# Small products of both heads claim their PSUM banks together, with new bank pools and a port rule in the planner

## Chip, cores and metric

One core of a Trainium2 chip runs the whole program. The metric is the device time of one execution in microseconds (us). The engines are TensorE (PE, its weight loads PEld), VectorE (DVE), ScalarE (ACT), GpSimd (POOL) and the DMA queue of SyncE (SP).

## What is computed

One mixer layer over 1024 tokens of width 1024, batch 1, all in fp32. An RMS norm and one wide projection feed two branches, a chunked gMLP and an RWKV-7 recurrence of 16 heads of 64; both are gated, merged and projected out.

```python
p = rms_norm(x, norm_pre_g) @ w_in
pa, pb, pg = p[..., :3072], p[..., 3072:7296], p[..., 7296:]
ya = gmlp_branch(pa, ...)      # u * (W_s LN(v) + b) * silu(z), blocks of 128 tokens
yb = rwkv7_branch(pb, ...)     # S_t = S_{t-1} diag(w_t) + (S_{t-1} (-kk_t)) (kk_t a_t)^T + v_t k_t^T ; o_t = S_t r_t
merged = sigmoid(pg[..., :1024]) * (ya @ w_branch_a) + sigmoid(pg[..., 1024:]) * (yb @ w_branch_b)
x = x + rms_norm(merged @ w_out, norm_post_g)
```

## The kernel before

**Dense products.** Large products are 128 x 128 weights against 512 columns. Each fp32 operand is split into a high and a low part (`whi`, `wlo`; `hm` for the activations), and three passes hi*hi, hi*lo, lo*hi are added in a `ps` bank. They run at the lowest priority, `DENSE`, in any gap of TensorE.

**Half-units.** `half_unit` handles the recurrence for one pair of heads and one half of the tokens: 8 pairs times 2 halves, 16 half-units, each with 8 chunks of 64 tokens. Head E lies in partitions 0 to 63, head O in 64 to 127. The small products of a half-unit stay in plain fp32, where one product is two records of TensorE in the trace (a transpose is one):

- `pg<-W,BK`: per chunk and head a 64-row product, each head into a bank of its own, four chunks to a bank; so two pairs of banks per half-unit, two times eight products. VectorE masks the banks into `Pm`, `BA` and `W`.
- An inversion of triangular blocks: `Pm` goes through DRAM into `B`, GpSimd runs a loop of 62 instructions (`qt<-B,Q` and `Q<-Q,qt`), the result comes back through DRAM as `N`, VectorE transposes it into `Pm` in four pieces, and 16 `N,Pm` and 16 `Pm,N` products finish it. Each of these two sets fills one `pm` bank.
- `pg<-con,v`, `pg<-con,BK`, `pg<-con,W`: centring and transposes over 128 rows.
- `X,Pm`: two times eight products; both heads write the same bank, at their own partitions.
- `BA,X`: like `W,BK`, two pairs of banks.
- `pc<-Z,W`: a chain of eight steps over the chunks, each carried on by ScalarE and VectorE; then `po<-W,Z`, 16 products into one `po` bank, which ends the half-unit on TensorE.
- Sums over heads (`head_sum`): ScalarE makes `sh`, GpSimd makes `sl` from it, TensorE multiplies both with `bdr`.

Buffers decide how far half-units overlap: `W` has 5 (two per half-unit, written at its beginning and read until its `po`), `Pm` and `BA` 2, `BK`, `B`, `Q`, `N` and `X` 1. Of the eight PSUM banks `ps` has 3, `pg` 2, `pm`, `po` and `pc` 1 each.

**Order.** `Sched` records all operations, then `flush` lists them per engine: it repeats choosing the ready operation that can start earliest, by costs from `cost`, and of equals the one with the smaller priority (`CHAIN` 0, `INV` 1, `PREP` 2.5, `LATE` 4, `DENSE` 9). `when` gives the time from which an operation's buffers are free. The engines then run their lists in that order, and wait on semaphores. Products of a `group_of` become ready together; `claim` names tiles that an operation must have before it starts.

**Stages.** Projections with `gp` tiles; the recurrent stage, in which the column tiles of the projections for the next heads and some of the `w_a` products are the dense work; the rest of `w_a`; and the last products (`product`, seven block products twice), for which VectorE and GpSimd split operands.

Of the kernel before, what the change touches and what calls it, by code (L numbers as in the profile page):

```python
# [11 lines left out]
F32 = mybir.dt.float32  # L12
F32R = mybir.dt.float32r
AF = mybir.ActivationFunctionType
# [4 lines left out]
P = 128  # L19
# [42 lines left out]
class Sched:  # L62
# [17 lines left out]
    def __init__(self, nc, tc=None, plan=None):  # L80
        self.nc, self.tc, self.plan = nc, tc, plan
        self.calls, self.cls, self.prio = [], [], 0
        self.ntile = self.nflush = 0
        self.PE, self.DVE, self.ACT, self.POOL, self.SP = (Queue(self, e) for e in self.ENGINES)
        self.names = {}
        self.group, self.bufs, self.slot = [], {}, []
        self.shape, self.dtype, self.used = [], [], []
        self.ops, self.orders, self.done = [], [], 0
        self.heirs, self.places = {}, {}
        self.hist, self.ends = {}, []  # L90
        self.free = dict.fromkeys(self.ENGINES, 0.0)
        self.hw = self.dq = 0.0
        self.table, self.array = None, (P, P)
        self.start, self.made = [], {}
# [27 lines left out]
    def call(self, eng, op, a, k):  # L122
# [8 lines left out]
        i = len(self.ops)  # L131
# [14 lines left out]
        if eng == "PE":  # L146
            size = (P, P) if op == "transpose" else (a[1].shape[0], a[1].shape[-1])
        self.ops.append((eng, deps, tiles, dur, (self.prio, i), table, size, op))

    cache = {}  # L150

    def region(self, ap, shape):

        sig = (tuple(shape), ap.offset, tuple(map(tuple, ap.ap)))
        if sig not in self.cache:
# [10 lines left out]
            self.cache[sig] = tuple(masks)  # L166
        return self.cache[sig]

    def cost(self, eng, op, a, k, outs, ins):
# [23 lines left out]
        if eng == "DVE":  # L193
            if op == "transpose":
                return 335, None, 0
            if op == "reciprocal":
                return 6.3 * n + 62, None, 0
            if op in ("bn_stats", "bn_aggr"):
                return (62 + ins[0].free_size()) / .96, None, 0
            if op in ("tensor_scalar", "tensor_copy") and not psum:  # L200
                n /= 2
            return (62 + n) / .96 + 63 * ptr, None, 0
# [9 lines left out]
    def flush(self):  # L212
# [38 lines left out]

        def when(t, i):
            for v in ops[i][2]:
                if v in where:
# [4 lines left out]
                    continue  # L259
                g = self.group[v]  # L260
                if self.bufs[g][1] and nxt[g][-1] != v:
                    return None
                s = state.setdefault(g, [])
                for h in [h for h in self.heirs.get(g, ()) if not nxt.get(h)]:
                    self.heirs[g].remove(h)
                    self.places[g] += [(h, k) for k in range(len(state[h]))]
                    s += state[h]
                if len(s) < self.bufs[g][0]:
                    continue
                f = [lastend[u] for u in s if not users.get(u)]  # L270
                if not f:
                    return None
                t = max(t, min(f))
            return t
# [5 lines left out]
        while len(order) < n - b0:  # L280
# [18 lines left out]
            ready[e] = [x for x in ready[e] if x[1] != i]  # L299
            eng, deps, tiles, dur, prio, table, size = ops[i][:7]  # L300
            for v in tiles:
# [18 lines left out]
            else:  # L320
# [6 lines left out]
                self.start[i] = s  # L327
                self.free[e] = ends[i] = s + dur
            order.append(i)
            for v in tiles:  # L330
# [53 lines left out]
def half_unit(S, I, rw, dram, bank, p, h, r, k0, v, zz, uh, ul, bdr, xw, xa, Z, KI, vec, con, hv, eps, yb):  # L384
# [76 lines left out]
    for c4 in range(2):  # L461
        cc = slice(4 * c4, 4 * c4 + 4)
        ps2 = [bank([P, 4, P], "pg") for _ in range(2)]
        with S.group_of():
            for j in range(4):
                for ps, e, hp in zip(ps2, (0, 1), (E, O)):
                    mm(ps[:, j, :], BK[hp, 4 * c4 + j, :], W2[c4][hp, j, :, e, :], start=True, stop=True,
                       claim=[Pm, BA])
        for ps, e, hp, other in zip(ps2, (0, 1), (E, O), (O, E)):
# [30 lines left out]
    py = bank([P, 8, 32], "pm")  # L500
    for c in range(8):
        for a in (0, 64):
            mm(py[a:a + 64, c, :], Pm[a:a + 32, c, :], N[a:a + 32, c, :], start=True, stop=True)
    Y = N
    V.tensor_scalar(Y, py, con[:, C_LOW:C_LOW + 1], None, op0=ALU.mult)
    p2 = bank([P, 8, 32], "pm")
    for c in range(8):
        for a in (0, 64):
            mm(p2[a:a + 32, c, :], Y[a:a + 64, c, :], Pm[a:a + 64, c, 32:64], start=True, stop=True)
    for a in (0, 64):  # L510
# [28 lines left out]
    for c4 in range(2):  # L539
# [5 lines left out]
        act(X[:, cc, :], px, AF.Copy)  # L545
    for c4 in range(2):
        cc = slice(4 * c4, 4 * c4 + 4)
        px = bank([P, 4, P], "pg")
        with S.group_of():
            for j in range(4):  # L550
                for hp in (E, O):
                    mm(px[hp, j, :], Pm[hp, 4 * c4 + j, :], X[hp, 4 * c4 + j, :], start=True, stop=True)
        act(X[:, cc, :], px, AF.Copy)

    for c4 in range(2):
        cc = slice(4 * c4, 4 * c4 + 4)
        ps2 = [bank([P, 4, P], "pg") for _ in range(2)]
        with S.group_of():
            for j in range(4):
                for ps, hp in zip(ps2, (E, O)):  # L560
                    mm(ps[:, j, :], X[hp, 4 * c4 + j, :], BA[hp, 4 * c4 + j, :], start=True, stop=True)
        for ps, e in zip(ps2, (0, 1)):
# [56 lines left out]
def trunk(S, enter, I, out):  # L619
# [31 lines left out]
    def bank(shape, name):  # L651
        bufs = {"ps": 3, "pg": 2, "pm": 1, "po": 1, "pc": 1}[name]
        return psum.tile(shape, F32, name=name, bufs=bufs, fifo=name in ("pc", "po", "pm"))

# [658 lines left out]
```

## Time and profile before

| | us |
|---|---|
| three runs, median (lowest to highest) | 1537.02 (1535.17 to 1548.76) |
| the profiled execution, time | 1538.7 |
| its span, first to last instruction | 1536.6 |
| TensorE busy in the span | 1433.5 (93%) |
| VectorE busy | 1058.2 (69%) |
| GpSimd busy | 905.6 (59%) |
| ScalarE busy | 732.6 (48%) |

Busy time of TensorE runs from a product's start to its modelled end, and products overlap, so the start-to-start distance in a timeline is what a product costs. A group of rows by line (`L127` is the recording helper, so nearly all operations carry it) is told apart by its tiles, `out<-in`. A wait is named after the operation that came last.

### The profile page before, as it was taken

How to read it: one execution, taken by the hardware profiler on the slowest of the kernel's cores; microseconds unless marked ns; L12 is line 12 of the kernel's file. 1: busy time of each engine (PE TensorE's matmuls, PEld its weight loads, DVE VectorE, ACT ScalarE, POOL GpSimd, SP SyncE). 2: the span in 40 equal slices, each digit the busy share in tenths (PEclk: the TensorE clock that was granted, in tenths of full speed). 3: DMA queues.
4: the chain of work that ended last, by engine and by line, in shares of the span. 5: the costliest groups of instructions: out<-in, count | busy, mean ns of one | idle time of the engine just before them, and what ended most of it. 6: DMA issues, size and time to landing. Idle time of an engine off the chain costs nothing. (4 is left out here: it accounts for less than half of the span.)

```text
span 1536.6 us, 23389 instructions
## 1 busy us (share of the span) xinstructions
PE 1433.5 (93%) x8390; PEld 1141.3 (74%) x8390; DVE 1058.2 (69%) x1764; ACT 732.6 (48%) x1334; POOL 905.6 (59%) x1405
## 2 busy tenths in 40 slices
PE   5999999999999999999999999989999999888796
PEld 3788788888887777777777777767777777666585
DVE  7868677753328576876867768658586745398977
ACT  5625443433336455655655555446555543043343
POOL 5554677764432665664664655647646562199686
PEclk9999999999999999999997999979999999999898
DMA  6104234433322111211122111111215744644032
GB/s 221 53 1 181 84 138 140 141 126 110 110 103 67 48 40 49 63 53 46 39 59 63 52 39 52 53 42 45 62 53 181 249 153 153 217 132 135 22 110 110
DMA packets 99155, 145.76 MB, mean 95 GB/s; under 512 B 42336, under 2 KB 52704, under 8 KB 99040
## 3 DMA queue, kind: packets, MB, share of 16 engines
q1 hardware_dynamic: 99040, 144.28, 28.7%
q8 instruction: 66, 1.08, 0.3%
q14 instruction: 49, 0.40, 0.1%
HBM read 106.49 MB, written 37.75 MB: 94 GB/s over the span
## 5 line engine op out<-in xcount | busy, mean ns | idle before, releaser
L127 PE MATMUL ps<-hm,whi 128*128 128x512 f32 x1616 | 549.0, 410 | 6.6 <-ACT whi L127 6.6
L127 PEld LDWEIGHTS ps<-hm,whi 128*128 128x128 f32 x1616 | 306.0, 193 | 71.1 <-ACT whi L127 7.0
L127 PE MATMUL ps<-hm,wlo 128*128 128x512 f32 x808 | 330.9, 410 | 0.0
L127 POOL TENSOR_TENSOR qt<-B,Q 128x60 f32<-128x60 f32 (+24 forms) x496 | 197.1, 397 | 83.0 <-DMA Q<-in_q_dram 34.7
L127 POOL TENSOR_TENSOR Q<-Q,qt 128x60 f32<-128x60 f32 (+24 forms) x496 | 183.3, 370 | 37.2
L127 PEld LDWEIGHTS ps<-hm,wlo 128*128 128x128 f32 x808 | 155.3, 192 | 33.2 <-issue 2.3
L127 ACT ACTIVATE whi<-raw 128x1024 fp32r<-128x1024 f32 x64 | 67.6, 1057 | 122.0 <-PE ps L127 69.5
L127 ACT ACT_TABLE_LOAD x69 | 88.5, 1283 | 1.9 <-PEq L1296 0.7
L127 PE MATMUL pg<-pg,ring 128*128 128x512 f32 x360 | 86.5, 389 | 0.0
L127 PE MATMUL pg<-W,BK 64*128 64x128 f32 (+1 forms) x521 | 76.5, 305 | 10.2 <-DVE W L127 4.6
L127 PEld LDWEIGHTS pg<-W,BK 64*128 64x128 f32 (+1 forms) x521 | 63.5, 203 | 29.5 <-issue 15.6
L127 POOL TENSOR_TENSOR wlo<-raw,whi 128x1024 fp32r<-128x1024 f32 x18 | 43.4, 2411 | 61.9 <-ACT whi L127 61.9
L127 PEld LDWEIGHTS pg<-pg,ring 128*128 128x128 f32 x360 | 67.6, 188 | 14.0
L127 ACT ACTIVATE Z<-pc,gc 64x64 f32<-64x64 f32 x120 | 36.7, 306 | 78.6 <-PE pc L127 71.8
L127 DVE TENSOR_TENSOR wlo<-raw,whi 128x1024 fp32r<-128x1024 f32 x46 | 58.2, 1265 | 20.3 <-ACT whi L127 19.6
L127 POOL TENSOR_TENSOR sl<-k,sh 128x512 fp32r<-128x512 f32 x16 | 23.9, 1496 | 74.7 <-ACT sh L127 74.7
L127 DVE TENSOR_SCALAR Z<-pc,gc 64x64 f32<-64x64 f32 x120 | 34.9, 291 | 43.5 <-ACT Z L127 28.6
L127 PE MATMUL pg<-BA,X 64*128 64x128 f32 x512 | 57.8, 289 | 0.3
L127 PEld LDWEIGHTS pg<-BA,X 64*128 64x128 f32 x512 | 46.9, 187 | 14.7 <-issue 7.9
L127 PE MATMUL ps<-pg,hm 128*128 128x512 f32 x192 | 53.1, 433 | 4.7 <-ACT hm L127 4.0
L127 ACT ACTIVATE X<-pg 128x512 f32<-128x512 f32 x64 | 37.4, 591 | 39.7 <-PE pg L127 39.3
L127 DVE TENSOR_TENSOR W<-pg,KI 128x256 f32<-128x256 f32 x64 | 26.9, 420 | 38.6 <-PE pg L127 38.4
(860 smaller groups left out, 3262.6 us busy)
## 6 DMA issues: line engine op xcount, KB each, us to landing
raw<-in_w_in_dram SPq DMA_DIRECT2D x65, 512.0 KB, 3.3
B<-bs_d SPq DMA_DIRECT2D x64, 128.0 KB, 2.6
hm<-ya_d SPq DMA_DIRECT2D x32, 256.0 KB, 5.4
raw<-in_w_a_dram SPq DMA_DIRECT2D x12, 512.0 KB, 3.9
sv<-sv_d SPq DMA_DIRECT2D x8, 512.0 KB, 3.3
ya_d<-th SPq DMA_DIRECT2D x8, 512.0 KB, 2.6
ya_d<-sv SPq DMA_DIRECT2D x8, 512.0 KB, 2.6
yb_d<-oc SPq DMA_DIRECT2D x16, 256.0 KB, 2.2
```

Of the source, the lines that this page charges most:

```text
L127: self.calls.append(lambda: getattr(e, op)(*a, **k))
```

## The change

1. `W,BK` and `BA,X` products claim both banks of their pair; a product cannot start until both are free, so that the list can take the heads in turn. `when` now asks for as many free buffers as an operation needs of a pool.
2. Both sets of `N,Pm` and `Pm,N` products become groups. `X,Pm` claims both of its banks and runs as one group.
3. The pools `pm` and `po` are dropped, `pg` has 4 banks and serves all three.
4. The planner knows the SBUF port that VectorE and GpSimd share: `shares` tells which operations use it (every GpSimd operation but a memset; on VectorE two SBUF inputs, or a copy or scalar operation within SBUF), and in the plan such an operation waits for the other engine's last one. No instruction comes of it. `tensor_tensor_scan` gets a cost of its own.

```diff
+        self.port = {"DVE": 0.0, "POOL": 0.0}
...
+    def shares(self, eng, op, outs, ins):
+
+        if eng == "POOL":
+            return op != "memset"
+        if eng != "DVE":
+            return False
+        sb = [x for x in ins if x.free_size() > 1 and self.group[self.names[x.tensor.name]][0] != "psum"]
+        if op in ("tensor_scalar", "tensor_copy"):
+            return len(sb) == 1 and self.group[self.names[outs[0].tensor.name]][0] != "psum"
+        return len(sb) > 1
...
+            if op == "tensor_tensor_scan":
+                return 2.23 * n, None, 0
...
         def when(t, i):
+            want = {}
...
+                want[g] = want.get(g, 0) + 1
                 if self.bufs[g][1] and nxt[g][-1] != v:
                     return None
+            for g, m in want.items():
...
-                if len(s) < self.bufs[g][0]:
+                m -= max(0, self.bufs[g][0] - len(s))
+                if m <= 0:
                     continue
-                f = [lastend[u] for u in s if not users.get(u)]
-                if not f:
+                f = sorted(lastend[u] for u in s if not users.get(u))
+                if len(f) < m:
                     return None
-                t = max(t, min(f))
+                t = max(t, f[m - 1])
+            if ops[i][8]:
+                t = max(t, self.port["POOL" if ops[i][0] == "DVE" else "DVE"])
             return t
...
+                if port:
+                    self.port[e] = s + dur
...
                     mm(ps[:, j, :], BK[hp, 4 * c4 + j, :], W2[c4][hp, j, :, e, :], start=True, stop=True,
-                       claim=[Pm, BA])
+                       claim=[Pm, BA, *ps2])
...
-    for c in range(8):
-        for a in (0, 64):
-            mm(py[a:a + 64, c, :], Pm[a:a + 32, c, :], N[a:a + 32, c, :], start=True, stop=True)
+    with S.group_of():
+        for c in range(8):
+            for a in (0, 64):
+                mm(py[a:a + 64, c, :], Pm[a:a + 32, c, :], N[a:a + 32, c, :], start=True, stop=True)
...
-    for c4 in range(2):
-        cc = slice(4 * c4, 4 * c4 + 4)
-        px = bank([P, 4, P], "pg")
-        with S.group_of():
-            for j in range(4):
-                for hp in (E, O):
-                    mm(px[hp, j, :], Pm[hp, 4 * c4 + j, :], X[hp, 4 * c4 + j, :], start=True, stop=True)
-        act(X[:, cc, :], px, AF.Copy)
+    px2 = [bank([P, 4, P], "pg") for _ in range(2)]
+    with S.group_of():
+        for c in range(8):
+            for hp in (E, O):
+                mm(px2[c // 4][hp, c % 4, :], Pm[hp, c, :], X[hp, c, :], start=True, stop=True, claim=px2)
+    for c4, px in enumerate(px2):
+        act(X[:, 4 * c4:4 * c4 + 4, :], px, AF.Copy)
...
-                    mm(ps[:, j, :], X[hp, 4 * c4 + j, :], BA[hp, 4 * c4 + j, :], start=True, stop=True)
+                    mm(ps[:, j, :], X[hp, 4 * c4 + j, :], BA[hp, 4 * c4 + j, :], start=True, stop=True, claim=ps2)
...
-        bufs = {"ps": 3, "pg": 2, "pm": 1, "po": 1, "pc": 1}[name]
-        return psum.tile(shape, F32, name=name, bufs=bufs, fifo=name in ("pc", "po", "pm"))
+        name = {"pm": "pg", "po": "pg"}.get(name, name)
+        bufs = {"ps": 3, "pg": 4, "pc": 1}[name]
+        return psum.tile(shape, F32, name=name, bufs=bufs, fifo=name == "pc")
```

The lists of TensorE show what comes of it. The first place is the `W,BK` products of the eighth half-unit, before; `pg_540` and `pg_541` are the banks of head E and head O for the first four chunks, `pg_542` the bank of head E for the last four.

```order
L127 MATMUL pg_540<-W_4870,BK_4880 128x128 x4
L127 MATMUL ps_539<-hm_1206,wlo_1077 128x512
L127 MATMUL ps_539<-hm_1208,whi_1076 128x512
L127 MATMUL ps_539<-hm_1212,whi_1076 128x512
L127 MATMUL pg_541<-W_4870,BK_4880 128x128 x4
L127 MATMUL ps_539<-hm_1208,wlo_1077 128x512
L127 MATMUL ps_539<-hm_1209,whi_1076 128x512
L127 MATMUL ps_539<-hm_1214,whi_1076 128x512
L127 MATMUL pg_542<-W_4891,BK_4880 128x128 x4
```

The same place of the change, the last four chunks (`pg_547` head E, `pg_548` head O):

```order
L128 MATMUL pg_547<-W_4902,BK_4890 128x128
L128 MATMUL pg_548<-W_4902,BK_4890 128x128
L128 MATMUL pg_547<-W_4902,BK_4890 128x128
L128 MATMUL pg_548<-W_4902,BK_4890 128x128
L128 MATMUL pg_547<-W_4902,BK_4890 128x128
L128 MATMUL pg_548<-W_4902,BK_4890 128x128
```

Before, four products of one head stand in a row, with dense products between the heads; now the heads take turns. The first four chunks (`pg_536`, `pg_537`) stand about 50 rows earlier in the list, in the same alternation but for one product that comes some rows later.

The second place is `BA,X` of the eleventh half-unit, before; `pg_689` is head E's bank, `pg_691` head O's.

```order
L127 MATMUL pg_688<-X_5028,Pm_5004 64x128 x8
L127 MATMUL pg_689<-BA_5005,X_5028 128x128 x4
L127 MATMUL ps_677<-hm_1217,whi_1100 128x512
L127 MATMUL ps_677<-hm_1220,whi_1100 128x512
L127 MATMUL ps_677<-hm_1217,wlo_1101 128x512
L127 MATMUL ps_690<-hm_1189,whi_1103 128x512
L127 MATMUL ps_690<-hm_1190,whi_1103 128x512
L127 MATMUL pg_691<-BA_5005,X_5028 128x128 x4
```

And of the change, where `pg_699` and `pg_701` are banks of head E, `pg_700` and `pg_702` of head O:

```order
L128 MATMUL pg_697<-X_5033,Pm_5004 64x128 x8
L128 MATMUL ps_693<-hm_1207,whi_1106 128x512
L128 MATMUL ps_693<-hm_1209,whi_1106 128x512
L128 MATMUL ps_693<-hm_1207,wlo_1107 128x512
L128 MATMUL ps_693<-hm_1210,whi_1106 128x512
L128 MATMUL pg_699<-BA_5003,X_5033 128x128
L128 MATMUL pg_700<-BA_5003,X_5033 128x128
L128 MATMUL pg_699<-BA_5003,X_5033 128x128
```

All sixteen `BA,X` products of the half-unit now follow each other in turn, where before they were four runs of four.

## Rows read from the trace of the kernel before

**Rows 1.** Windows: length, then busy (instructions) by engine, PEclk, DMA, GB/s.

```profile
0.00:482.00 482.00, 460.18 (x2035) 377.27 (x2035) 305.07 (x465) 209.55 (x389) 266.42 (x195) 0.99 0.33 115
482.00:1290.00 808.00, 769.32 (x5507) 601.21 (x5507) 559.26 (x1089) 436.76 (x784) 472.57 (x1104) 0.96 0.24 73
1290.00:1339.00 49.00, 40.47 (x175) 31.85 (x172) 18.79 (x22) 11.57 (x14) 4.75 (x3) 0.93 0.68 234
1339.00:1537.00 198.00, 163.49 (x685) 130.97 (x683) 175.08 (x189) 74.74 (x149) 161.85 (x103) 0.92 0.30 100
```

**Rows 2.** Groups of PE by shape: records | busy us, mean ns | idle before.

```profile
L127 PE MATMUL pg<-W,BK 64*128 64x128 f32 x512 | 73.9, 304 | 10.2 <-DVE W L127 4.6 <-ACT KI L127 2.1 <-DVE BK L127 1.8
L127 PE MATMUL pg<-BA,X 64*128 64x128 f32 x512 | 57.8, 289 | 0.3
L127 PE MATMUL pg<-X,Pm 64*64 64x128 f32 x512 | 33.6, 277 | 1.1 <-ACT KI L127 0.5 <-DVE bon L127 0.3 <-DVE sq L127 0.2
L127 PE MATMUL pm<-N,Pm 32*64 32x32 f32 x512 | 30.7, 236 | 9.5 <-DVE Pm L127 9.3
L127 PE MATMUL pm<-Pm,N 64*32 64x32 f32 x512 | 13.4, 211 | 0.0
```

**Rows 3.** Timeline of PE in the eleventh half-unit: start us, us, operation, records.

```profile
1037.35 1.09 PE L127 MATMUL pg<-X,Pm 64*64 64x128 f32 x16 [0.24 <-DVE sq L127]
1038.37 1.16 PE L127 MATMUL pg<-BA,X 64*128 64x128 f32 x8
1039.46 0.73 PE L127 MATMUL ps<-hm,whi 128*128 128x512 f32 x2
1040.03 0.39 PE L127 MATMUL ps<-hm,wlo 128*128 128x512 f32 x1
1040.26 0.63 PE L127 MATMUL ps<-hm,whi 128*128 128x512 f32 x2
1040.82 1.16 PE L127 MATMUL pg<-BA,X 64*128 64x128 f32 x8
```

**Rows 4.** Timeline of PE, a run of `W,BK` in the sixteenth half-unit.

```profile
1204.92 1.24 PE L127 MATMUL pg<-W,BK 64*128 64x128 f32 x16
1206.09 1.15 PE L127 MATMUL po<-W,Z 128*64 128x64 f32 x32
```

**Rows 5.** Timeline of PE, a run of `N,Pm` in the third half-unit.

```profile
632.35 2.00 PE L127 MATMUL pm<-N,Pm 32*64 32x32 f32 x32
634.28 0.50 PE L127 MATMUL pg<-sh,bdr 128*128 128x512 f32 x1
```

**Rows 6.** Longest waits of PE, 482 to 1290: us in total, times, longest.

```profile
PE pg L127 <- POOL sl L127: 10.1, 8, 3.5
PE pm L127 <- DVE Pm L127: 9.3, 14, 2.2
```

**Rows 7.** Timeline of POOL (two rows) and of DVE at one time.

```profile
695.18 0.35 POOL L127 TENSOR_TENSOR qt<-B,Q 128x68 f32<-128x68 f32 x1
...
696.02 1.22 POOL L127 TENSOR_TENSOR qt<-B,Q 128x64 f32<-128x64 f32 x1
...
695.81 1.23 DVE L127 TENSOR_TENSOR wlo<-raw,whi 128x1024 fp32r<-128x1024 f32 x1 [0.44 <-ACT whi L127]
```

**Rows 8.** Timeline of PE: the loop from the eighth to the tenth half-unit.

```profile
904.08 1.15 PE L127 MATMUL po<-W,Z 128*64 128x64 f32 x30
...
922.34 1.91 PE L127 MATMUL pg<-W,BK 64*128 64x128 f32 x16
...
981.79 1.61 PE L127 MATMUL pm<-N,Pm 32*64 32x32 f32 x32
...
1004.62 1.15 PE L127 MATMUL po<-W,Z 128*64 128x64 f32 x32
```

**Rows 9.** Timeline of PE between the last half-unit and the last products.

```profile
1325.49 1.22 PE L127 MATMUL ps<-hm,whi 128*128 128x512 f32 x2 [6.57 <-ACT whi L127]
...
1338.87 0.85 PE L127 MATMUL ps<-BA,xa 128*128 128x512 f32 x3
```

More of the change, by code (lines that the diff above doesn't have):

```diff
@@ L147, in call @@
             size = (P, P) if op == "transpose" else (a[1].shape[0], a[1].shape[-1])
-        self.ops.append((eng, deps, tiles, dur, (self.prio, i), table, size, op))
+        self.ops.append((eng, deps, tiles, dur, (self.prio, i), table, size, op, self.shares(eng, op, outs, ins)))
     cache = {}
@@ L299, in flush @@
             ready[e] = [x for x in ready[e] if x[1] != i]
-            eng, deps, tiles, dur, prio, table, size = ops[i][:7]
+            eng, deps, tiles, dur, prio, table, size, _, port = ops[i]
             for v in tiles:
@@ L506, in half_unit @@
     p2 = bank([P, 8, 32], "pm")
-    for c in range(8):
-        for a in (0, 64):
-            mm(p2[a:a + 32, c, :], Y[a:a + 64, c, :], Pm[a:a + 64, c, 32:64], start=True, stop=True)
+    with S.group_of():
+        for c in range(8):
+            for a in (0, 64):
+                mm(p2[a:a + 32, c, :], Y[a:a + 64, c, :], Pm[a:a + 64, c, 32:64], start=True, stop=True)
     for a in (0, 64):
@@ L545, in half_unit @@
         act(X[:, cc, :], px, AF.Copy)
-    for c4 in range(2):
-        cc = slice(4 * c4, 4 * c4 + 4)
-        px = bank([P, 4, P], "pg")
-        with S.group_of():
-            for j in range(4):
-                for hp in (E, O):
-                    mm(px[hp, j, :], Pm[hp, 4 * c4 + j, :], X[hp, 4 * c4 + j, :], start=True, stop=True)
-        act(X[:, cc, :], px, AF.Copy)
+    px2 = [bank([P, 4, P], "pg") for _ in range(2)]
+    with S.group_of():
+        for c in range(8):
+            for hp in (E, O):
+                mm(px2[c // 4][hp, c % 4, :], Pm[hp, c, :], X[hp, c, :], start=True, stop=True, claim=px2)
+    for c4, px in enumerate(px2):
+        act(X[:, 4 * c4:4 * c4 + 4, :], px, AF.Copy)
     for c4 in range(2):
```

## Prediction

> **What bounds the kernel now.** First the busy time by stage [rows 1]. The program has four stretches: projections that need no small products (0 to 482 us), the recurrent stage with the small products of 16 half-units (482 to 1290), what is left of the dense products of `w_a` (1290 to 1339), and the last products (1339 to the end). In the recurrent stage TensorE is busy 769 of 808 us, VectorE 559, ScalarE 437, GpSimd 473. So TensorE carries the stage: it is idle 38.7 us, and its granted clock of 0.96 there means that about 8% of the stage ran at the lower of the two levels, which lost about 32 us. Dense products have the lowest priority in the planner and fill every gap, so TensorE's work, not one dependency, is the first thing to count.
>
> Next the groups of TensorE by shape [rows 2]. Each of the kinds listed there has 512 records, two for a product, so 256 products in 16 half-units. `pg<-W,BK` costs 73.9 us, `pg<-BA,X` 57.8, but `pg<-X,Pm`, which also streams 128 columns through 64 rows, only 33.6. The timeline shows why [rows 3, 4]. In `X,Pm` the heads alternate, since both write one bank: eight products start at 1037.35 and the next kind starts at 1038.37, 1.02 us. `BA,X` writes a bank for each head, and here the program has four products of one head alone: 1038.37 to 1039.46, 1.09 us for four; the other head's four start at 1040.82. Where the banks happened to be free together the heads alternate there too: eight `W,BK` products take 1204.92 to 1206.09, 1.17 us [rows 4].
>
> **The change part by part.** *Banks claimed at once.* The order of the built programs gives the counts. Products that follow one of the same head inside a run: `W,BK` 146 before and 0 after, `BA,X` 72 and 0. A broken bank pair has six such steps, so these are 24 + 12 = 36 broken pairs of 64. A broken pair costs two runs of 1.09 us, each with a lead-in: the two dense products that start at 1040.26, at the 0.23 us from 1040.03 to 1040.26, would let the next start at 1040.72, and it starts at 1040.82, so 0.10 us [rows 3]. That is 2 x 1.19 = 2.38. An alternating run costs 1.17 + 0.10 = 1.27. Each pair saves 1.11 us, 36 pairs 40 us.
>
> *Fewer runs.* Entries into one of the six small kinds from another array shape fall from 189 to 134. Of these 55, 36 are counted above. For the other 19 no row shows a run's fixed cost alone; it lies between the 0.10 us lead-in and the 0.5 us by which a run of four (1.09) exceeds half an alternating run of eight (0.58). I take 0.3, so 6 us (2 to 10).
>
> *`N,Pm` as a group.* The order has 98 same-head steps in it before and none after. It costs 30.7 us, `Pm,N`, alternating already, 13.4 [rows 2]; one half-unit's run lasts from 632.35 to 634.28, 1.93 us [rows 5]. Of the 17.3 us difference 9.3 are waits for VectorE's four transposes [rows 6], which a group only gathers into one wait ahead of it. The gain is between 0 and 8 us; I take 5, nearer the upper end because runs without a wait are slow as well.
>
> That `N,Pm` gains at all although both heads write one bank is read from `X,Pm`: one bank, eight products, 1.02 us [rows 3]. The Trainium skill, TensorEngine Tiling (Array Packing), section Restrictions and Gotchas, says that different row tiles cannot access the same PSUM bank at the same time. By that rule this gain would be nothing and the sum 46 in place of 51. The trace disagrees with it here, since alternating in one bank costs no more than alternating over two.
>
> *`X,Pm` over two banks in one run, `pm` and `po` out of the `pg` pool.* The bank count stays at eight. `X,Pm` is entered 23 times for 20, under 1 us. The dense and last stages keep their products. Cost nothing, hidden by TensorE's own stream; if a bank were missing, the price would show as a wait of TensorE for an evacuation, and its two longest waits are of another kind [rows 6].
>
> *The shared port in the planner.* It adds no instruction, but reorders VectorE and GpSimd everywhere. That the two do block each other is seen at 695.81: VectorE's `wlo` runs 1.23 us, and GpSimd's `qt` that starts at 696.02 takes 1.22 in place of 0.35 [rows 7]. The old plan did not know this, so TensorE's order expects GpSimd early and waits 10.1 us for `sl` and 9.3 for the transposes behind GpSimd's loop [rows 6]. A truer plan can give back up to these 19 us; a worse order can cost as much. Outside the recurrent stage it could add or remove one wait of the last stage, where TensorE idles 34.5 us [rows 1]; I take both as 0, with about 10 us either way.
>
> *Sum.* 40 + 6 + 5 = 51 us of TensorE's work. As an upper bound, `W,BK` and `BA,X` at the price of `X,Pm` give 40.3 + 24.2, with 8 for `N,Pm` 72; the lower bound is the first term alone, 40. TensorE is busy 95% of the stage, so I let it all reach the end, with idle time and clock loss as they are. The profiled execution took 1538.7 us, 1.7 over the median of 1537.0: 1487.7 by its own time, **1486** against the median.
>
> **The rivals.**
>
> *The chain of half-units sets the pace.* A half-unit needs the `W` buffers of the one two before it. Their loop reads: last product of one, `po`, at 904.08; `W,BK` of the second next at 922.34; `N,Pm` at 981.79 behind GpSimd's triangular inversion; `po` at 1004.62 [rows 8]. That is 100.5 us for two half-units, the same as the stage's 808 / 8 = 101, so the loop is as tight as TensorE's work is. If it holds its length, freed TensorE time is filled with dense products only. The order shows what then happens: 739 dense products stand behind the last `po`, 846 before, so 107 x 0.23 = 24.6 us leave the tail; the `w_a` remainder there shrinks from 160 products to 53. The recurrent stage stays at 808: 1514 against the profiled run, **1512** against the median. For it: the loop's length. Against it: small products are on the loop as well, 51 / 16 = 3.2 us a half-unit. The Trainium skill, the same page, section Performance Considerations, warns that evacuation of PSUM becomes the bottleneck once tiling has made TensorE faster, which would end here too. The trace bears that out little: VectorE is busy 69% of the stage [rows 1].
>
> *The waits go as well.* If the truer plan removes the waits of [rows 6], 51 + 19 = 70 us: **1467**.
>
> *The new order stretches the loop: slower.* Between the first and the last `W,BK` product of a half-unit stand 10 dense products before and 30 after (means of the order): +20 x 0.23 = 4.6 us. Between the last and `N,Pm` 131 and 165: +7.8. From there to `po` 6 fewer: -1.4. With 3.2 us off for the small products, a loop grows by 7.8 us if the order sets its length; eight loops +62, less 24.6 of the tail, +37: **1574**. It is slower than before by over 1% once loops grow by 5 us (8 x 5 = 40 = 24.6 + 15.4). Against it: `W,BK` to `N,Pm` took 59 us from first to first [rows 8], far more than the dense products in it, so the inversion sets it and the added ones fill time in which TensorE had slower small products and waits.
>
> **How the numbers follow.** Forecast (1470 to 1505) 60%; waits go too (1455 to 1470) 12%; the loop sets the pace (1505 to 1521) 16%; gains and losses of the order cancel (1521 to 1552) 7%; slower rival 5%. The range 1458 to 1518 takes in the 72 us bound and most of the loop's case, and leaves out about 2 in 10. One per cent, 15 us, is about what a measurement of this kernel can tell from no change: faster 0.87, same 0.08, slower 0.05.
>
> **What would show it.** In the profile after: `pg<-W,BK` and `pg<-BA,X` near 36 to 45 us each, in runs of 16 records of about 1.2 us; `N,Pm` near 25; TensorE's busy time in the recurrent stage lower by about 51 less the 24 us of dense products moved in; from the last `po` to the first of the last products about 25 us in place of 49 [rows 9], with the 6.57 us wait for a `w_a` load perhaps still in it. The waits for `sl` show whether the port rule matters. If the small products shrink as said but TensorE's idle time grows by 25 us or more, the loop was the bound. If `W,BK` stays above 60 us, alternation was not what made it dear and the sum is wrong.

## The result: 1487.46 us, and the profile after

The changed kernel takes 1487.46 us (median of four runs, 1484.92 to 1489.99). The kernel before, timed again beside it, takes 1541.04; the ratio is 0.9649, 95% interval 0.9596 to 0.9703. The forecast was 1486. One execution of the kernel before and one of e12 below, which took more than twice as long as the others (3413 and 3147 us), are left out of every figure here.

The profile after by stage, in the four stretches of [rows 1] and with the same columns; the borders are the first `W,BK`, the last `po` (now `pg<-W,Z`) and the first of the last products:

```profile
0.00:494.30 494.30, 462.16 (x2037) 375.69 (x2037) 297.32 (x466) 215.11 (x392) 270.84 (x195) 0.99 0.32 112
494.30:1256.60 762.30, 718.06 (x5613) 567.20 (x5614) 565.91 (x1102) 438.41 (x786) 458.25 (x1104) 0.96 0.28 85
1256.60:1269.40 12.80, 12.80 (x65) 10.55 (x61) 5.99 (x7) 7.98 (x11) 4.21 (x3) 1.00 0.18 68
1269.40:1487.30 217.90, 164.68 (x685) 131.69 (x683) 164.67 (x190) 75.45 (x149) 154.10 (x103) 0.88 0.34 112
```

The recurrent stage is 45.7 us shorter and the remainder of `w_a` 36.2, but the projections are 12.3 us and the last products 19.9 us longer: -49.7 in all between the two profiled executions (the medians differ by 53.6). The total that was forecast is thus made of gains larger than forecast and of losses that were not forecast.

TensorE's groups by shape, which answer to [rows 2]:

```profile
L128 PE MATMUL pg<-W,BK 64*128 64x128 f32 x512 | 41.7, 287 | 0.0
L128 PE MATMUL pg<-BA,X 64*128 64x128 f32 x512 | 35.1, 280 | 0.0
L128 PE MATMUL pg<-X,Pm 64*64 64x128 f32 x512 | 34.3, 275 | 0.0
L128 PE MATMUL pg<-N,Pm 32*64 32x32 f32 x512 | 22.9, 233 | 7.9 <-DVE Pm L128 7.7
```

`W,BK` gave 32.2 us, `BA,X` 22.7, `N,Pm` 7.8: 62.7. `X,Pm`, now one run over two banks, costs what it did (33.6). The timeline of the eleventh half-unit shows the new form, to be held against [rows 3]:

```profile
1016.23 1.74 PE L128 MATMUL pg<-X,Pm 64*64 64x128 f32 x26
1017.89 0.73 PE L128 MATMUL ps<-hm,whi 128*128 128x512 f32 x2
1018.46 0.39 PE L128 MATMUL ps<-hm,wlo 128*128 128x512 f32 x1
...
1019.02 2.06 PE L128 MATMUL pg<-BA,X 64*128 64x128 f32 x32
1021.00 0.51 PE L128 MATMUL ps<-hm,whi 128*128 128x512 f32 x1
```

All sixteen `BA,X` products of the half-unit start at 1019.02 and the next dense product at 1021.00: 1.98 us, 2.08 with the lead-in of 0.10 that the run has here as well. Before they were four runs of 1.09 with a lead-in of 0.10 each, 4.76 us.

TensorE's waits in the recurrent stage, answering to [rows 6] (us in total, times, longest):

```profile
PE pg L128 <- ACT sh L128: 26.8, 7, 8.4
PE pg L128 <- DVE Pm L128: 7.7, 6, 4.6
...
PE pg L128 <- POOL sl L128: 1.7, 2, 1.1
```

The waits for `sl` (10.1 before) are nearly gone, and waits for ScalarE's `sh` have come. The longest of them on TensorE:

```profile
858.02 1.16 PE L128 MATMUL pg<-W,BK 64*128 64x128 f32 x16
859.12 0.50 PE L128 MATMUL ps<-hm,wlo 128*128 128x512 f32 x1
859.45 0.39 PE L128 MATMUL pg<-sl,bdr 128*128 128x512 f32 x1
868.20 0.79 PE L128 MATMUL pg<-sh,bdr 128*128 128x512 f32 x1 [8.36 <-ACT sh L128]
```

Behind `W,BK` stand one dense product and one of `sl`, and then TensorE's list has nothing before the product of `sh`: it has no dense product at this place, though it has more of them later (the next starts at 873.84).

In the last stage TensorE's waits are 40.3 us in five, where they were 21.0 in three; the two longest after, and the longest before:

```profile
PE ps L128 <- POOL wlo L128: 21.0, 1, 21.0
PE ps L128 <- DVE raw L128: 11.2, 1, 11.2
```

```profile
PE ps L127 <- DVE wlo L127: 9.8, 1, 9.8
```

And GpSimd, which makes the `wlo` of the longest, stands still for 11.57 us ahead of it: the next operation in its list waits for VectorE's `Pm`.

```profile
1372.39 2.86 POOL L128 TENSOR_TENSOR hm<-hm,hm 128x512 f32<-128x512 f32 x2 [11.57 <-DVE Pm L128]
...
1383.26 1.71 POOL L128 TENSOR_TENSOR wlo<-hm,wlo 128x512 fp32r<-128x512 f32 x1
```

### The profile page after: what moved, and what is told of

Same layout as the page of the kernel before. It is cut to its first block, busy times and chain, and to the rows that moved or that the text cites. A ratio compares the mean times of both kernels' runs of the same rounds, so it can differ in the third digit from the quotient of the medians.

```text
span 1487.3 us, 23327 instructions
## 1 busy us (share of the span) xinstructions
PE 1357.7 (91%) x8390; PEld 1085.1 (73%) x8390; DVE 1033.9 (70%) x1764; ACT 737.0 (50%) x1336; POOL 887.4 (60%) x1405
## 5 line engine op out<-in xcount | busy, mean ns | idle before, releaser
L128 PE MATMUL ps<-hm,whi 128*128 128x512 f32 x1616 | 538.5, 405 | 2.2 <-ACT whi L128 1.6
L128 PE MATMUL ps<-hm,wlo 128*128 128x512 f32 x808 | 326.3, 405 | 0.1
L128 POOL TENSOR_TENSOR qt<-B,Q 128x60 f32<-128x60 f32 (+24 forms) x496 | 185.3, 374 | 107.2 <-DMA Q<-in_q_dram 32.0
L128 PE MATMUL pg<-pg,ring 128*128 128x512 f32 x720 | 171.1, 391 | 5.7 <-ACT ring L128 3.7
L128 PEld LDWEIGHTS pg<-pg,ring 128*128 128x128 f32 x720 | 134.1, 188 | 37.7 <-ACT ring L128 6.4
L128 POOL TENSOR_TENSOR wlo<-raw,whi 128x1024 fp32r<-128x1024 f32 x18 | 45.5, 2525 | 58.5 <-ACT whi L128 56.7
L128 ACT ACTIVATE Z<-pc,gc 64x64 f32<-64x64 f32 x120 | 36.7, 306 | 81.6 <-PE pc L128 80.3
L128 PE MATMUL ps<-pg,hm 128*128 128x512 f32 x192 | 53.6, 439 | 10.0 <-ACT pg L128 3.7
L128 PEld LDWEIGHTS ps<-pg,hm 128*128 128x128 f32 x192 | 40.0, 212 | 22.6 <-ACT pg L128 4.4
L128 PE MATMUL pc<-Z,W 128*128 128x128 f32 x240 | 50.8, 293 | 2.4 <-DVE W L128 1.6
L128 PEld LDWEIGHTS pc<-Z,W 128*128 128x128 f32 x240 | 38.9, 188 | 18.2 <-DVE Z L128 7.8
L128 POOL TENSOR_TENSOR sl<-k,sh 128x512 fp32r<-128x512 f32 x16 | 22.7, 1417 | 44.0 <-ACT sh L128 42.9
L128 PE MATMUL pg<-W,BK 64*128 64x128 f32 (+1 forms) x530 | 46.8, 290 | 0.6 <-DVE r L128 0.6
L128 PE MATMUL pg<-sh,bdr 128*128 128x512 f32 x48 | 22.8, 475 | 26.9 <-ACT sh L128 26.8
```

The lines of the kernel that those rows point to most:

```text
L128: self.calls.append(lambda: getattr(e, op)(*a, **k))
```

## The experiments

Three questions: is it the small products, is it the port rule, and which part of each. The table has the times and the stages (length in us of the projections, the recurrent stage, the remainder of `w_a`, the last products, from each profile). The kernel before was timed beside every group of runs, at 1540.1 to 1542.6. A gain or loss below is a difference of medians; the differences between stages are of the profiled executions.

| kernel | us | ratio to before, 95% | stages |
|---|---|---|---|
| before | 1541.0 | | 482.3, 807.8, 48.8, 197.8 |
| the change | 1487.5 | 0.965 (0.960 to 0.970) | 494.3, 762.3, 12.8, 217.9 |
| e1, no port rule | 1479.6 | 0.961 (0.958 to 0.964) | 485.6, 754.4, 42.0, 198.1 |
| e2, port rule alone | 1505.1 | 0.977 (0.973 to 0.980) | 482.9, 805.4, 17.8, 200.0 |
| e5, pools alone | 1490.2 | 0.969 (0.965 to 0.972) | 485.6, 756.0, 48.6, 198.0 |
| e3, rule in the recurrent stage alone | 1463.4 | 0.950 (0.948 to 0.953) | 485.9, 759.5, 18.0, 198.6 |
| e9, rule everywhere but in the last products | 1472.5 | 0.956 (0.951 to 0.961) | 496.8, 758.7, 18.0, 198.7 |
| e10, e3 with the heads apart | 1486.9 | 0.965 (0.961 to 0.970) | 486.0, 781.6, 18.9, 199.2 |
| e11, e3 without claims | 1464.1 | 0.951 (0.947 to 0.954) | 485.3, 760.1, 13.5, 202.2 |
| e12, e3 without the group of `N` | 1474.0 | 0.958 (0.954 to 0.963) | 485.1, 767.8, 16.4, 201.2 |
| e15, pools and rule, no claims, no groups | 1481.1 | 0.959 (0.955 to 0.963) | 486.7, 776.5, 14.6, 202.0 |
| e14, no rule, dearer GpSimd | 1464.0 | 0.949 (0.944 to 0.953) | 486.5, 764.2, 6.7, 204.3 |
| e16, e3 and dearer GpSimd | 1552.2 | 1.006 (1.004 to 1.009) | 487.1, 857.2, 4.3, 206.2 |
| e13, e3 with two buffers for `r` | 1460.2 | 0.946 (0.943 to 0.950) | 486.5, 756.9, 14.6, 201.5 |

**The change without the port rule (e1).**

```diff
-            if ops[i][8]:
+            if False:
```

> The changed kernel without the port rule in the planner; banks, claims and groups stay, so no small product follows one of its own head and TensorE's small products should cost what they cost in the changed kernel (W,BK about 42 us, BA,X 35, N,Pm 23). Theory A (small products give the gain, about 51 us of TensorE's work; the port rule gave some 30 us more in the recurrent stage and its remainder of w_a by fewer waits, and lost 12 us before and 20 us after it by another order): stages about 482, 808+49-51 = 806, 198, so 1488 +- 10, with the wait for sl back near 10 us. Theory B (the port rule's order is the main source, and the cheaper small products only filled time that was idle anyway): 1515 or more.

1479.6 us, as theory A: faster than the whole change by 7.9, and the four runs of each do not overlap. The small products (`W,BK` 44.3, `BA,X` 35.8, `N,Pm` 20.3) give 62.0 us of TensorE's time against before, and the end moves by 61. So the small products carry the gain, and the rule as a whole costs. The stage rows (recurrent stage, remainder):

```profile
485.60:1240.00 754.40, 707.14 (x5523) 550.44 (x5522) 554.49 (x1089) 432.50 (x781) 473.01 (x1104) 0.97 0.27 80
1240.00:1282.00 42.00, 36.71 (x156) 28.51 (x151) 18.77 (x21) 11.33 (x14) 5.07 (x3) 0.96 0.68 241
```

The gain lies in the recurrent stage; the remainder is still 42.0 of 48.8. The waits for `sl`, which theory A put near 10 us, have grown to 22.1 there:

```profile
PE pg L128 <- POOL sl L128: 22.1, 14, 3.0
```

**The port rule alone (e2).** The kernel before with `shares`, the port's lines in `when` (with them those that count free buffers) and the price of the scan, the rule on in the recurrent stage only; pools and order of the products as before. What the price of the scan and the count give by themselves was not run; e1 and e3 differ by the rule alone.

```diff
+            if ops[i][8]:
+                t = max(t, self.port["POOL" if ops[i][0] == "DVE" else "DVE"])
...
+        S.rule = True
...
+        S.rule = False
```

> The kernel before with nothing but the port rule and the scan's cost, in force in the recurrent stage only. Its order has 322 products that follow one of the same head (316 before), so W,BK and BA,X stay near 74 and 58 us. Theory A: recurrent stage and w_a remainder together shorter by the 30 us that the forecast's 51 left unexplained, so about 1508. Theory B: nearly the whole gain of these stages, 80 us, so about 1460. Theory C (the rule does nothing, the 81 us are all small products and banks): 1537.

1505.1, as theory A: it gains 36 us by itself, with the dear small products (`W,BK` 65.5, `BA,X` 57.0). The stage rows:

```profile
482.90:1288.30 805.40, 768.77 (x5594) 602.08 (x5593) 565.41 (x1100) 440.86 (x787) 454.79 (x1104) 0.97 0.27 80
1288.30:1306.10 17.80, 17.80 (x85) 14.30 (x82) 7.56 (x9) 9.01 (x12) 4.61 (x3) 1.00 0.33 116
```

The recurrent stage keeps its length, 805.4, and the remainder falls from 48.8 to 17.8. By the lists, 760 dense products stand behind the last `po`, 846 before: 86 have moved into gaps of the recurrent stage. That is the shape of the rival in which only the tail shrinks, and it is the rule that makes it, not the small products.

**The pools alone (e5).**

```diff
-        bufs = {"ps": 3, "pg": 2, "pm": 1, "po": 1, "pc": 1}[name]
-        return psum.tile(shape, F32, name=name, bufs=bufs, fifo=name in ("pc", "po", "pm"))
+        name = {"pm": "pg", "po": "pg"}.get(name, name)
+        bufs = {"ps": 3, "pg": 4, "pc": 1}[name]
+        return psum.tile(shape, F32, name=name, bufs=bufs, fifo=name == "pc")
```

> The kernel before with nothing but the new bank pools (pg 4 banks, pm and po gone). Four free banks already let the heads alternate more often: 138 same-head steps in its order in place of 316, and 129 entries into small kinds in place of 189. Priced with the rows of before, that is 39 of the 51 us. Theory A: 1537 - 39 = 1498. If the claims are what matters: about 1525 or more. If the pools also end waits for banks that the sum put at nothing: under 1490.

1490.2, 8 us better than theory A: the pools alone give 51 us. `W,BK` falls to 48.4 and `BA,X` to 43.6 with no claim in the program; products of one head in a row fall from 146 to 34 and from 72 to 42.

**The rule in the recurrent stage alone (e3).**

```diff
+        self.rule = False
...
-        self.ops.append((eng, deps, tiles, dur, (self.prio, i), table, size, op, self.shares(eng, op, outs, ins)))
+        self.ops.append((eng, deps, tiles, dur, (self.prio, i), table, size, op, self.rule and self.shares(eng, op, outs, ins)))
...
+        S.rule = True
...
+        S.rule = False
```

> The changed kernel with the port rule in force in the recurrent stage only, not in the projections before it nor in the last products. If the rule's order is what cost 12 us before the recurrent stage and 20 us in the last products, and its gain lies between: 482 + 762 + 13 + 198, about 1457. If the two losses come from the banks (pm and po now in pg, fewer different banks in turn): no change, about 1487.

1463.4, 24 us faster than the change. Against e1, which has no rule, the recurrent stage is 5.1 us longer and the remainder 24.0 shorter: by the lists 761 dense products stand behind the last `po` for 831, and 70 x 0.23 = 16.1 us have moved; the remainder's idle time, 5.3 us in e1, is gone as well. Rows for the recurrent stage, the remainder and the last stage:

```profile
485.90:1245.40 759.50, 713.98 (x5591) 563.32 (x5592) 562.79 (x1100) 437.50 (x785) 459.23 (x1104) 0.96 0.28 85
1245.40:1263.40 18.00, 18.00 (x86) 14.50 (x82) 8.30 (x9) 9.14 (x12) 4.06 (x3) 1.00 0.36 127
1263.40:1462.00 198.60, 162.49 (x685) 130.28 (x684) 175.01 (x190) 74.93 (x149) 161.77 (x103) 0.92 0.36 120
```

The last products have their old length again, and the projections nearly. (They take 485 to 487 us in every run with the new pools and no rule in that stage, and 482 to 483 with the old pools; why was not looked into.) In the last stage VectorE is busy 10 us longer than in the change (175.0 for 164.7) and GpSimd 8 (161.8 for 154.1), which fits their blocking each other again, and yet the stage is 19 us shorter: kept apart by the plan, the two engines lose more by standing still than they lose by blocking.

**The rule everywhere but in the last products (e9).** As e3, with `self.rule = True` from the start.

> The changed kernel with the port rule off for the last products only, so in force in the projections and in the recurrent stage. If the rule costs some 8 us in the projections and 20 in the last products: 1487 - 20 = 1468 to 1471, with the recurrent stage beginning near 494. If all of the loss is in the last products: 1463, beginning near 486.

1472.5, so the rule costs 9.0 us in the projections (against e3) and 15.0 in the last products (against the change). With e1 the rule's three parts are -16.1, +9.0 and +15.0: +7.9.

**Heads apart (e10).** e3, with the loop over the heads outside, so that four products of a head stand in a row, but the run of sixteen whole.

```diff
-            for j in range(4):
-                for ps, hp in zip(ps2, (E, O)):
+            for ps, hp in zip(ps2, (E, O)):
+                for j in range(4):
```

> The fastest run so far (port rule in the recurrent stage only, 1463) with one thing undone: in W,BK and BA,X the four products of head E come first, then the four of head O, in the same two banks claimed together. Banks, claims, groups and planner stay. Same-head steps 369 in place of 0, entries into small kinds 144 in place of 133. If alternation itself is the price (theory A, by the rows of before +45 us of TensorE): W,BK back to about 65 us, BA,X to about 57, and 1508. If TensorE has slack in this stage (the loop of half-units or waits set the pace): W,BK and BA,X as dear, but 1483 or less.

1486.9, between the two theories: alternation is worth 23.4 us. `W,BK` costs 59.0 and `BA,X` 48.2, together 30.8 more than in e3, which is less than the 45 that I had expected; TensorE's idle time in the stage fell from 45.5 to 36.7, so not all of it reached the end. The same place as above:

```profile
1021.27 2.82 PE L129 MATMUL pg<-BA,X 64*128 64x128 f32 x32
1024.02 0.51 PE L129 MATMUL ps<-hm,wlo 128*128 128x512 f32 x1
```

Sixteen products take 2.75 us here and 1.98 when they alternate, 2.85 and 2.08 with the lead-in of 0.10, and 4.76 before, as four runs apart. So of 2.68 us saved at this place only 0.77 is alternation; 1.91 comes of the runs no longer being broken up by dense products.

**No claims (e11).** e3, with `claim=[Pm, BA]` for `W,BK` and no claim for `BA,X`.

> The same fastest kernel without the claims of two banks for W,BK and BA,X; four pg banks, groups and port rule stay. Its order has 12 same-head steps and 156 entries in place of 0 and 133, 8 us of TensorE by the rows of before. If the claims are needed for what the forecast gave them (40 us for alternation): 1490 or more. If the pool of four banks already does it: about 1470.

1464.1, the same as e3. With four banks in one pool both banks are nearly always free by the time a pair begins: the list has no product of one head behind another in `W,BK` and 12 in `BA,X` (40.2 us for 35.1). The claims are not what brings the gain.

**No group for `N,Pm` and `Pm,N` (e12).** e3 without the two `with S.group_of()` ahead of them.

> The same fastest kernel with the two sets of products on N no longer grouped: 110 same-head steps in N,Pm come back. The forecast gave the group 5 us (0 to 8): N,Pm from 23 us back to about 28, and 1468. If the four transposes come late anyway, the ungrouped products run while the last transposes are made: no change, 1463.

1474.0 (1472.3 to 1483.4), 10.6 us slower, twice the term of the sum. `N,Pm` costs 28.7 for 22.9, the waits for `Pm` grow from 7.9 to 10.8, and the recurrent stage is 8.3 us longer. Not all of that is the group: `W,BK`, `BA,X` and `X,Pm`, which the edit does not touch, cost 5.9 us more as well, and the last products are 2.6 longer and the remainder 1.6 shorter, by nothing but another plan.

**Pools and rule without claims and groups (e15).** The kernel before with the edits of e5 and of e2.

> The kernel before with four banks in one pool and the port rule in the recurrent stage, without the claims and without the products of N, Pm and the two X banks as one group. Pools alone gave 1490 us, the rule alone 1505. If what these two give adds up (47 to 51 us by the pools, 30 to 36 by the rule) 1456 to 1462 us, and claims and groups are worth nothing; if the claims and the groups earn what the runs without each of them suggest together (1 us by the claims, 13 by the group of N) about 1475 us; if pools and rule share one gain, 1485 us or more.

1481.1: not additive (1456 to 1462), and between the other two forecasts. Claims and groups, with the one run of `X,Pm`, are worth 17.7 us together; the claims alone 0.7 and the group of `N` 10.6. The recurrent stage is 17 us longer than e3's, with `N,Pm` at 30.3.

**A dearer GpSimd in place of the rule (e14).** The inversion is 992 small tensor operations of GpSimd. Two things of them can be read from the trace of before (timeline of POOL: start, us):

```profile
699.84 0.34 POOL L127 TENSOR_TENSOR Q<-Q,qt 128x65 f32<-128x65 f32 x1
700.25 0.32 POOL L127 TENSOR_TENSOR qt<-B,Q 128x60 f32<-128x60 f32 x1
700.65 0.31 POOL L127 TENSOR_TENSOR Q<-Q,qt 128x60 f32<-128x60 f32 x1
```

They last 0.31 to 0.34 us and follow each other at 0.40 to 0.41. The plan counts 2.1 ns an element and 152 ns, 0.28 us at 60 elements. Some 0.125 us are missing from each, by this estimate 992 x 0.125 / 16 = 7.8 us of every half-unit's inversion.

```diff
-            return 2.1 * n + 152, None, 0
+            return (2.2 * n + 265 if n < 128 else 2.1 * n + 152), None, 0
```

> The change without the port rule anywhere (1480 us when it was run), but with the plan's time for a small GpSimd tensor operation raised to what the trace of before shows for one (a pitch of 0.40 to 0.41 us at 60 to 65 elements, where the plan counts 0.28). Theory A: what the rule gains in the recurrent stage is only that the plan counts GpSimd's time there more truly (the rule makes the Q loop's instructions later), so a dearer price alone gives the same: about 1463 us, with the stretch to the first last product 18 us or less where it was 42. Theory B: it takes the exclusion itself, VectorE and GpSimd not planned at once: about 1480 us, and that stretch stays near 42 us. By the order alone 712 dense products stand behind the first of the last half-unit's outputs, where 831 did and with the rule 761, so A is likelier.

1464.0 with no port rule at all, the time of e3, by other stages: the remainder, 6.7 us, is 11.3 shorter than e3's, the recurrent stage 4.7 and the last products 5.7 longer. So a gain as large as the rule's needs no exclusion; a plan that counts GpSimd's inversion longer gives as much. That the rule works by the same means, in that it makes the inversion wait for VectorE in the plan, is my reading.

**Both (e16).** e3 with that price as well.

> The change with the port rule in the recurrent stage alone (1463 us) and the raised GpSimd price as well. If the price and the rule stand for the same thing, 1463 us within 6 either way; if the plan still counts GpSimd too cheaply under the rule, 1450 to 1457 us, out of the recurrent stage (759 us) and the stretch to the first last product (18 us); if GpSimd's work is then counted twice, so that the dense products are handed out too early, 1470 us or more, with more of the waits in which dense products have run out (26.8 us on sh).

1552.2, slower than before by 0.6%, with the cheap small products (`W,BK` 42.3, `BA,X` 38.7). The recurrent stage:

```profile
487.10:1344.30 857.20, 765.78 (x5666) 606.21 (x5667) 565.55 (x1107) 446.69 (x793) 444.68 (x1106) 0.92 0.26 77
```

TensorE is idle 91.4 us there, 45.5 in e3, the waits for `sh` are 38.6 us in 16 for 26.8 in 7, as the third theory has it, and the granted clock is 0.92 for 0.96. The first `W,BK` of the third and of the fifteenth half-unit, in e16 and then in e3, give the loop:

```profile
567.62 0.94 PE L129 MATMUL pg<-W,BK 64*128 64x128 f32 x12
...
1163.98 1.16 PE L129 MATMUL pg<-W,BK 64*128 64x128 f32 x14
```

```profile
556.36 0.93 PE L129 MATMUL pg<-W,BK 64*128 64x128 f32 x10
...
1105.63 1.16 PE L129 MATMUL pg<-W,BK 64*128 64x128 f32 x16
```

(1163.98 - 567.62) / 6 = 99.4 us for two half-units, against 91.5. And the timeline of e16 in between:

```profile
1069.82 0.49 PE L129 MATMUL pc<-Z,W 128*128 128x128 f32 x2 [1.09 <-DVE Z L129]
1071.57 0.49 PE L129 MATMUL pc<-Z,W 128*128 128x128 f32 x2 [1.26 <-ACT Z L129]
...
1082.65 0.72 PE L129 MATMUL pg<-sl,bdr 128*128 128x512 f32 x1 [1.94 <-POOL sl L129]
1086.69 0.80 PE L129 MATMUL pg<-sh,bdr 128*128 128x512 f32 x1 [3.32 <-ACT sh L129]
```

Between 1068 and 1087 the list has no dense product at all: the chain of `Z`, `sl` and `sh` runs bare, with a wait at each link. My reading is that the plan, with the inversion counted too long, puts the dense products elsewhere; what the runs show is the bare stretch and the longer loop.

**Two buffers for `r` (e13).** e3 with a buffer less for a tile of the dense chain, to see whether its buffers make the waits for `sh`.

```diff
-            return rw.tile([P, 512], F32, name="r", bufs=3)
+            return rw.tile([P, 512], F32, name="r", bufs=2)
```

(and `halves("r", 3)` to 2).

> The change with the port rule in the recurrent stage alone (1463 us), with two buffers instead of three for the tile r of the dense chain. After the change TensorE's waits in this stage are for ScalarE's sh (26.8 us), in places where the dense products have run out. Theory A: the buffers of the dense chain limit how far the dense products run ahead, so that what the shorter small products give back is partly lost there: with a buffer less the recurrent stage is 15 us or more longer than 759 us, and those waits grow. Theory B: the chain through VectorE, ScalarE and GpSimd itself is the limit there, and not the buffers: within 5 us of 759 us.

1460.2, the recurrent stage 756.9: theory A falls for this tile. The waits for `sh` stay (24.7 us in 8). What stands in the 8.36 us ahead of 868.20 in the change is seen on ScalarE: three table loads of 1.28 between its other operations.

```profile
860.01 1.28 ACT L128 ACT_TABLE_LOAD   x1
...
863.70 1.28 ACT L128 ACT_TABLE_LOAD   x1
...
865.70 1.28 ACT L128 ACT_TABLE_LOAD   x1
...
867.53 0.61 ACT L128 ACTIVATE sh<-k 128x512 fp32r<-128x512 f32 x1
```

That these loads are the cause was not tried.

The versions e13, e3, e14 and e11 (1460 to 1464) beat both kernels, by 5% against before; which of the four is best is near the limit of what the runs can tell. Of their edits only the rule of e3 and the price of e14 were tried together (e16).

## Why the prediction was right, and where it was not

**The small products.** Right that they shrink, low in size, and right in mechanism only in part: `W,BK` and `BA,X` were to give 40 + 6 and gave 54.9. What was mis-sized is the second term. I read the price of a broken pair as four products of one head, so as the lack of alternation, and put 0.3 us on a run of its own. e10 shows that alternation gives 30.8 us of TensorE's time over 369 steps of one head in its list, 0.083 us a step (seven more runs are in it, so this is rather high). At that price the 218 such steps of before make 18 of the 55.3 us by which its two kinds cost more than those of e3; the other 37 fall on 51 more runs of these two kinds (112 for 61), an estimate of 0.73 us each, and the same sum for e2 (46.1 us, 216 steps worth 18, 53 runs more) gives 0.53. So the 19 runs of the second term are worth some 10 to 14 us and not 6, and by these estimates some two thirds of the 55.3 are that runs stay whole. That no row shows a run's fixed cost alone holds no longer: eight alternating products take 1.10 us (858.02 to 859.12) and sixteen 1.98, so 0.22 of a run does not grow with its products; with 0.10 ahead of it and 0.11 in the dense product behind it, 0.43 us is my estimate of that part. The Trainium skill, TensorEngine Tiling (Array Packing), section Key Properties, says that a change of the tiling mode drains the TensorE; it gives no figure, and the trace agrees in kind: the first dense product behind a run shows 0.50 or 0.51 us where others show 0.39.

**Claims and pools.** Wrong. The forecast gave the 40 us to the claims and put the pools at nothing. It is the other way round: the pools alone give 51 us (e5) and the claims nothing once the pools are there (e11). The order of the built program showed what changed, not which edit made it.

**`N,Pm`.** 5 us were taken of 0 to 8; TensorE's row fell by 7.8 in the change, and e12 moved the end by 10.6, of which `N,Pm` itself is 5.8 and its waits 2.9. The bound of 8 was misread: the 9.3 us of waits for the transposes stand beside the 30.7 us of busy time [rows 2], not in it, so the difference of 17.3 was the bound, and e1, with `N,Pm` at 20.3, gained 10.4. Alternation within one bank does pay. The rule against it, by which the term would be nothing (the Trainium skill, TensorEngine Tiling (Array Packing), section Restrictions and Gotchas), does not show in these traces: `N,Pm` fell from 30.7 to 22.9, and stands at 28.7 in e12, whose list has 110 steps of one head in it again.

**All of it reaches the end.** Right: in e1 62.0 us of products move the end by 61. TensorE's idle time in the recurrent stage hardly changed (38.7 before, 44.2 after), but by other waits.

**The port rule at 0.** The failed step. Its sum, +7.9 us, lies in the bounds given (19 in the stage, 10 outside it), so the time came out, but it is -16 by the recurrent stage and the remainder, +9 in the projections and +15 in the last products: 24 outside, where the bound was 10. I asked which wait the rule would take away and did not ask what the rule costs where VectorE and GpSimd are the bound: in the last stage they are busy 175 and 162 of 198 us [rows 1], and a plan that keeps them apart has no room. The 62.7 us of small products less 7.9 would be 54.8; the measured difference is 53.6. That the forecast of 1486 lies so near to 1487.5 is thus luck in good part: small products 11.7 us better than the 51 taken, and a rule 7.9 worse than nothing.

**What would show it.** `W,BK` and `BA,X` near 36 to 45, `N,Pm` near 25: as said. The remainder was to be 25 us and is 12.8, but by the rule (42.0 without it, in e1); the wait of 6.57 us [rows 9] is gone. TensorE's busy time in the recurrent stage was to fall by 27 and fell by 51.3 [rows 1]. The three kinds give 62.7, `po` and `Pm,N` 3.5 more, and the dense products moved in take 24.6: 41.6. Some 6 of the other 10 us can be the shorter first dense products behind 55 fewer runs (55 x 0.11, an estimate); the rest stays open.

**The rivals.** The loop as the pace: it did not hold its length. Two half-units take (1150.61 - 564.62) / 6 = 97.7 us before and (1113.01 - 564.75) / 6 = 91.4 after:

```profile
564.62 1.40 PE L127 MATMUL pg<-W,BK 64*128 64x128 f32 x16
...
1150.61 1.16 PE L127 MATMUL pg<-W,BK 64*128 64x128 f32 x8
```

```profile
564.75 0.93 PE L128 MATMUL pg<-W,BK 64*128 64x128 f32 x10
...
1113.01 0.93 PE L128 MATMUL pg<-W,BK 64*128 64x128 f32 x10
```

6.3 us less is twice 3.1, about the 3.2 a half-unit that small products have on the loop. Near `sh` the loop may bound (26.8 us of waits), so this rival can hold for a few places; but with the list of e14 these waits are 8.7 us, so they are the list's doing as well. The waits that were to go went, `sl` from 10.1 to 1.7, and others came. The slower rival, a list that stretches the loop, did not come with this change, but e16 is that case: 99.4 us a pair, and slower than before. Evacuation is not the bound either: VectorE is busy 566 of 762 us. The Trainium skill, TensorEngine Tiling (Array Packing), section Performance Considerations, is weaker than the prediction puts it: after a fourfold speed-up of TensorE the copy out of PSUM may become the bottleneck. No run here shows that.

## What to carry to other kernels

Look for small products that dense work breaks up: keeping a run whole was worth more here than the order inside it, and one pool of four banks did it without any claim. Where a planner sets a static order, read its prices against the trace before giving it a new rule; here a truer price for one engine's small operations gave as much as the rule in its best place, and both together lost 89 us against either. And when an edit acts on the whole program, cost it in every stage, above all in the one where the engines it touches are the bound.

## What the runs showed of the hardware

Products of two heads on different rows, in blocks of four of one head behind four of the other, still overlap in part: sixteen take 2.75 us, against 1.98 in turn. VectorE and GpSimd do block each other where both read two SBUF inputs: in the last stage of the change a 128x512 operation of VectorE takes 0.68 us while GpSimd stands still, and 1.75 beside GpSimd's. Keeping them apart cost more than that blocking: that stage is 19 us longer with the rule than without (15 at the end, since the remainder of `w_a` is 5 shorter).

```profile
1371.63 0.68 DVE L128 TENSOR_TENSOR Pm<-hm,hm 128x512 f32<-128x512 f32 x1
...
1381.59 1.71 POOL L128 TENSOR_TENSOR Z<-sh,Z 128x512 fp32r<-128x512 f32 x1
...
1382.10 1.75 DVE L128 TENSOR_TENSOR whi<-r,whi 128x512 fp32r<-128x512 f32 x1
```
